# A driver that merges streams by modelled engine times instead of written-out latencies

## The chip, the cores and the metric

The kernel runs on one core of a Trainium2 chip. Its engines are named as in the profile: PE is TensorE (matmuls; PEld is its loading of weights), DVE is VectorE, ACT is ScalarE, POOL is GpSimd, SP is SyncE, which issues most DMAs. The metric is device time in microseconds from start to end of one execution, as a median of several runs.

## The reference

Three layers run on 512 positions of width 1024, in fp32. The first mixes grouped-query attention with a bidirectional gated delta rule; the second and the third are a stick-breaking attention and a differential attention, each with a SwiGLU feed-forward behind it.

```python
def first_block(x, p, ...):
    h = rms_norm(x, norm_pre[i])
    (aq, ak, av, az, dq, dk, dv, db, da, dz, gate_att, gate_dn) = split_cols(h @ w_in[i])
    o_att = gqa_attention(q, k, v)               # q, k normed per head, rotated
    qkv = silu(short_conv(concat([dq, dk, dv]), conv_w[i]))
    o_dn = bidir_gated_deltanet(qd, kd, vd, g, beta)   # chunks of 64, state carried
    mix = (sigmoid(gate_att) * y_att + sigmoid(gate_dn) * y_dn) @ w_out[i]
    x = x + rms_norm(mix, norm_post[i])
    return x + rms_norm(sigmoid(x @ w_ple_gate[i]) * (p[i] @ w_ple_proj[i]), ple_norm[i])

def stick_breaking_attention(q, k, v):           # 16 heads of 64
    z = einsum('bqhd,bkhd->bhqk', q_blk, k) * scale
    log_keep = where(earlier, log_sigmoid(-z), 0.0)
    log_after = cumsum(log_keep, reverse=True) - log_keep
    weight = where(earlier, exp(log_sigmoid(z) + log_after), 0.0)
    return einsum('bhqk,bkhd->bqhd', weight, v)

def differential_attention(q1, q2, k1, k2, v, lam):
    a = softmax(mask(q1 @ k1)) - lam * softmax(mask(q2 @ k2))
    return a @ v

x = x + mixer(rms_norm(x)); x = x + (silu(h @ w_gate) * (h @ w_up)) @ w_down   # twice
```

## The kernel before

Activations stay on chip, with features on partitions and the 512 positions as columns (or the other way round where a stage wants it). A matmul of fp32 accuracy is made of three passes over values split into a high and a low part (hi, lo), so a projection is three times 8 matmuls of 512 columns for each 128 outputs. Weights come by DMA, and ScalarE and VectorE split them into whi and wlo.

The order of the program is made in Python while the kernel is built. Each piece of work (a projection, an attention unit, a chain of the delta rule) is a generator, a stream, and `Driver.run` (L116) merges the streams. The driver has one clock, `drv.t`, which each matmul or transpose moves on by its cost (`mm`, L293; `transpose`, L303). A stream that yields a number is ready again so much later; one that yields an `Event` is ready when the event has been set, at the time in it; one that yields a pool of slots (`self.free["z"]`: PSUM banks for z) waits for a free one. Among the streams the driver takes the one that is ready first, and among equals the one that stands first in the list. The latencies of VectorE and ScalarE are constants, written by hand: SB_LAT1 = 5.0 and SB_LAT2 = 1.2 in the stick-breaking units, CH1 to CH3 = 1.3 in the delta rule's chain, and so on. A scheduler of the framework then places instructions on each engine; an engine runs its instructions in the order that results.

The stages, in order of time: the first block (to about 885 us of the span), the start of the stick-breaking projections (to 921), the stick-breaking units with the rest of their projections (to 1147), the end of the output projection (to 1179), a feed-forward (to 1542), the differential stage (to 1821), a feed-forward.

In the first block, streams project q, k, v of the attention (paq, pak, pv in the trace), z, and dq, dk, dv of the delta rule; `conv` (L831) takes a projection of these out of its PSUM bank on ScalarE (cacc) and runs the short convolution on VectorE; `dn_prep` (L858) transposes the results on TensorE (tr) and multiplies them (kk, kq); `dn_inv` (L959) inverts the triangular matrices; `dn_chain` (L1126) carries the state (kS, wS).

The stick-breaking stage has 48 units, for 8 pairs of heads, 2 heads, and three blocks of keys (b = 2, 1, 0; b = 2 holds two blocks, in 384 columns, b = 1 one in 384, b = 0 one in 512). The `unit` of `stick` (L694) does:

```python
            if prev:
                yield prev["S"]
            yield self.free["z"]
...
                self.mm(zz, kh[:, ks], q[:, P * i:], j == 0, False)
...
            self.split(sh[:, :n], sl[:, :n], t, act=False)
...
            drv.set(me["S"])
            yield SB_LAT1
...
            w = self.work("w")[:, :n]
            nc.scalar.activation(out=w, in_=zz, func=AF.Exp)
            drv.release(self.free["z"], SB_LAT2)
            yield SB_LAT2
```

Called A here are its first matmuls (z from qs with kh and kl, and a mask); then follow Abs, Exp and Ln on ScalarE (L714 to L716, tile t), and on VectorE a sum (L717), sh (L319) and sl (L320). Called B are the matmuls of sh and sl with negones and m_ntri, which add the reversed cumulative sum into z; then Exp on ScalarE gives w (L733), and C are the matmuls po from w and v. The projections of the stage (pv, sb_q, sb_k) are one more stream, last in the list, and the output projection (po0, po1 from ohi and olo) follows them there. In the differential stage, `unit` (L1910) is built in the same manner, with softmax; its output os is transposed on TensorE (otr).

Of the kernel before, what the change touches and what calls it, by code (L numbers as in the profile page):

```python
# [79 lines left out]
class Event:  # L80
    def __init__(self):
        self.t = None
# [14 lines left out]
class Driver:  # L97
# [2 lines left out]

    def __init__(self):
        self.t = 0.0

    def set(self, ev, lat=0.0):
        ev.t = self.t + lat

    def release(self, slots, lat=0.0, n=1):
        slots.free.extend([self.t + lat] * n)  # L110

    def spawn(self, g):

        self.tasks.insert(0, [g, self.t, None])

    def run(self, streams):  # L116
        tasks = self.tasks = [[g, 0.0, None] for g in streams]
        while tasks:
            best = None
            for k, (g, ready, need) in enumerate(tasks):  # L120
                if isinstance(need, Event):
                    if need.t is None:
                        continue
                    ready = max(ready, need.t)
                elif isinstance(need, Take):
                    if len(need.slots.free) < need.n:
                        continue
                    ready = max(ready, sorted(need.slots.free)[need.n - 1])
                key = (max(ready, self.t), k)
                if best is None or key < best[0]:  # L130
                    best = (key, k)
            if best is None:
                raise RuntimeError("streams wait for each other: " + str([(g.__name__, n) for g, _, n in tasks]))
            task = tasks[best[1]]
            self.t = max(self.t, best[0][0])
            g, _, need = task
            if isinstance(need, Take):
                need.slots.free.sort()
                del need.slots.free[:need.n]
            try:  # L140
                v = next(g)
            except StopIteration:
                tasks.remove(task)
                continue
            if isinstance(v, Slots):
                v = Take(v, 1)
            if isinstance(v, (Event, Take)):
                task[1:] = self.t, v
            else:
                task[1:] = self.t + (v or 0.0), None  # L150


class Raw:
# [14 lines left out]
class Net:  # L168
    def __init__(self, ctx, tc, ins, out):
        self.tc = tc  # L170
        self.nc = tc.nc
        self.ins = ins
        self.out = out
        self.drv = Driver()
        self.pre = None
        self.nw = 0

# [57 lines left out]

    def drop(self, n, lat=0.0):

        self.drv.release(self.mem, lat, n)

    def need(self, n):  # L240
        return Take(self.mem, n)
# [16 lines left out]
    def consts(self):  # L258
        nc = self.nc
        self.ident = self.cp.tile([P, P], F32, name="ident")  # L260
        make_identity(nc, self.ident)
# [31 lines left out]
    def mm(self, out, lhsT, rhs, start, stop):  # L293
        n = 1
        for d in rhs.shape[1:]:
            n *= d
        if lhsT.dtype == F32R:
            self.drv.t += max(n * 0.42, 106 if lhsT.shape[-1] == P and lhsT.shape[0] == P else 54) / 1000
        else:
            self.drv.t += max(n * 1.67, 108) / 1000  # L300
        self.nc.tensor.matmul(out, lhsT=lhsT, rhs=rhs, start=start, stop=stop, skip_group_check=True)  # L301

    def transpose(self, out, in_):  # L303
        self.drv.t += 0.109
        self.nc.tensor.transpose(out, in_, self.ident)

    def mm3(self, out, ls, rs, start, stop):
# [14 lines left out]
    def wtile(self, ap, n=1024):  # L322

        nc = self.nc
        with self.tc.high_priority(offset=self.woff):
            st = self.wst.tile([P, 1024], F32, tag="st", name="st")
            nc.sync.dma_start(out=st[:, :n], in_=ap)
            self.nw += 1
            third = self.w3 is not None and self.nw % 4 == 0
            hi = (self.w3 if third else self.whi).tile([P, 1024], F32R, tag="hi", name="whi")  # L330
            lo = (self.w3 if third else self.wlo).tile([P, 1024], F32R, tag="lo", name="wlo")
            self.split(hi[:, :n], lo[:, :n], st[:, :n])
        return hi, lo

    def wtile_big(self, ap):

        nc = self.nc
        parts = []
        with self.tc.high_priority(offset=WBOFF):
            for j in range(2):  # L340
                st = self.work("wbst")
                BQ(nc).dma_start(out=st, in_=ap[:, j * T:(j + 1) * T])
                hi, lo = self.chunk("wbhi", F32R), self.chunk("wblo", F32R)
                self.split(hi, lo, st)
                parts.append((hi, lo))
        return parts

# [778 lines left out]
    def dn_chain(self, S, hh, d):  # L1126
# [13 lines left out]
        for step in range(4):  # L1140
# [4 lines left out]
            if step:  # L1145
# [1016 lines left out]
```

## Time and profile before

| | |
|---|---|
| median of 3 runs | 2192.55 us (2190.63 to 2194.14) |
| the profiled execution | 2189.46 us |
| its span, first to last instruction | 2187.7 us |
| mean granted clock of TensorE | 0.986 |
| busy: PE, DVE, ACT, POOL | 2101.1, 1234.3, 991.6, 115.7 us |
| first block, 0 to 885 us: PE busy | 823.26 us |
| stick-breaking units, 921 to 1147 us: PE busy | 223.89 us |
| differential stage, 1542 to 1821 us: PE busy | 260.69 us |

Busy is the time in which an engine has an instruction under way; matmuls overlap in TensorE's pipeline, so a single matmul's duration (some 0.39 us for 512 columns) is longer than its step to the next. The clock is a share of TensorE's full 2.4 GHz, 0.50 being 1.2 GHz. A row's "<-" in square brackets names what ended the idle time ahead of it.

### The profile page before, as it was taken

How to read it: one execution, taken by the hardware profiler on the slowest of the kernel's cores; microseconds unless marked ns; L12 is line 12 of the kernel's file. 1: busy time of each engine (PE TensorE's matmuls, PEld its weight loads, DVE VectorE, ACT ScalarE, POOL GpSimd, SP SyncE). 2: the span in 40 equal slices, each digit the busy share in tenths (PEclk: the TensorE clock that was granted, in tenths of full speed). 3: DMA queues.
4: the chain of work that ended last, by engine and by line, in shares of the span. 5: the costliest groups of instructions: out<-in, count | busy, mean ns of one | idle time of the engine just before them, and what ended most of it. 6: DMA issues, size and time to landing. Idle time of an engine off the chain costs nothing.

```text
span 2187.7 us, 32571 instructions
## 1 busy us (share of the span) xinstructions
PE 2101.1 (96%) x12830; PEld 1783.9 (82%) x12830; DVE 1234.3 (56%) x2487; ACT 991.6 (45%) x2001; POOL 115.7 (5%) x157
## 2 busy tenths in 40 slices
PE   7999899899999999899999999999999989999999
PEld 6788788778788877788878888888999968888887
DVE  8865774786542546755555444433577765444421
ACT  6556556555632345566664222222466544222211
POOL 2000000000000000000000000000111100000000
PEclk9999999998999999899999999999999999999999
DMA  4221021131324353011103222333211112222332
GB/s 156 75 80 53 32 80 50 46 93 47 117 88 145 130 174 104 20 49 58 48 31 107 96 96 97 94 92 99 91 50 50 57 58 94 95 95 97 92 112 71
DMA packets 73994, 181.68 MB, mean 83 GB/s; under 512 B 24177, under 2 KB 24817, under 8 KB 73841
## 3 DMA queue, kind: packets, MB, share of 16 engines
q1 hardware_dynamic: 72560, 175.40, 25.0%
q0 software_dynamic: 1280, 4.20, 0.6%
q8 instruction: 101, 1.65, 0.3%
q14 instruction: 53, 0.43, 0.1%
HBM read 170.13 MB, written 9.44 MB: 82 GB/s over the span
## 4 chain that ended last, share of the span: by engine, by line
PE 80%; DVE 11%; ACT 4%; issue 2%; POOL 2%; DMA 0%; SPq 0%; POOLq 0%; DVEq 0%; ACTq 0%
PE pg L301 17%; PE pd L301 11%; PE pu L301 11%; PE po L301 9%; PE pb L301 4%; PE pv L301 3%; PE z L301 3%; PE pz L301 3%; PE pk L301 2%; PE wS L301 2%; DVE cacc L845 2%; PE sb_q L301 2%; PE sb_k L301 1%; PE s L301 1%; DVE wlo L320 1%
## 5 line engine op out<-in xcount | busy, mean ns | idle before, releaser
L317 ACT CAST whi<-st 128x1024 fp32r<-128x1024 f32 (+1 forms) x295 | 306.2, 1040 | 787.7 <-issue 343.3
L320 DVE TENSOR_TENSOR wlo<-st,whi 128x1024 fp32r<-128x1024 f32 (+1 forms) x295 | 356.5, 1210 | 281.6 <-ACT whi L317 276.8
L301 PE MATMUL pg<-rlo,whi 128*128 128x512 f32 x352 | 138.7, 394 | 0.0
L301 PE MATMUL pg<-rhi,whi 128*128 128x512 f32 x352 | 138.1, 392 | 0.0
L301 PE MATMUL pg<-rhi,wlo 128*128 128x512 f32 x352 | 138.0, 392 | 0.0
L301 PE MATMUL pd<-mh,wlo 128*128 128x512 f32 x352 | 137.5, 391 | 0.0
L301 PE MATMUL pd<-mh,whi 128*128 128x512 f32 x352 | 137.5, 391 | 0.0
L301 PE MATMUL pd<-ml,whi 128*128 128x512 f32 x352 | 137.5, 391 | 0.0
L301 PE MATMUL pu<-rhi,wlo 128*128 128x512 f32 x352 | 137.2, 390 | 0.0
L301 PE MATMUL pu<-rlo,whi 128*128 128x512 f32 x352 | 137.1, 389 | 0.0
L301 PE MATMUL pu<-rhi,whi 128*128 128x512 f32 x352 | 136.9, 389 | 0.0
L2030 DVE TENSOR_TENSOR sg<-pg,rfm 128x512 f32<-128x512 f32 x44 | 30.4, 692 | 118.4 <-PE pg L301 118.3
L2036 DVE TENSOR_TENSOR m<-pu,sg 128x512 f32<-128x512 f32 x44 | 30.4, 692 | 115.4 <-PE pu L301 115.4
L845 DVE SCALAR_TENSOR_TENSOR cacc<-craw,convw,cacc 128x510 f32<-128x510 f32 (+1 forms) x96 | 70.2, 746 | 17.6 <-ACT cacc L841 16.7
L301 PE MATMUL pv<-whi,rhi 128*128 128x256 f32 x256 | 76.6, 299 | 3.3 <-ACT tmq L1848 2.1
L301 PEld LDWEIGHTS pg<-rhi,wlo 128*128 128x128 f32 x352 | 66.2, 188 | 15.1 <-issue 0.5
L301 PEld LDWEIGHTS pg<-rlo,whi 128*128 128x128 f32 x352 | 66.3, 188 | 15.0 <-issue 0.5
L301 PEld LDWEIGHTS pg<-rhi,whi 128*128 128x128 f32 x352 | 66.2, 188 | 14.5
L301 PEld LDWEIGHTS pd<-ml,whi 128*128 128x128 f32 x352 | 66.2, 188 | 14.3
L301 PEld LDWEIGHTS pd<-mh,wlo 128*128 128x128 f32 x352 | 66.1, 188 | 14.2
L301 PEld LDWEIGHTS pd<-mh,whi 128*128 128x128 f32 x352 | 66.1, 188 | 14.2
L301 PEld LDWEIGHTS pu<-rlo,whi 128*128 128x128 f32 x352 | 66.1, 188 | 14.0
(563 smaller groups left out, 5679.7 us busy)
## 6 DMA issues: line engine op xcount, KB each, us to landing
st<-w_gate SPq DMA_DIRECT2D x44, 512.0 KB, 3.3
st<-w_up SPq DMA_DIRECT2D x44, 512.0 KB, 3.3
st<-w_down SPq DMA_DIRECT2D x32, 512.0 KB, 3.5
st<-w_dn SPq DMA_DIRECT2D x24, 512.0 KB, 3.4
st<-w_out SPq DMA_DIRECT2D x24, 512.0 KB, 3.4
st<-w_down SPq DMA_DIRECT2D x16, 384.0 KB, 3.2
x<-xT SPq DMA_DIRECT2D x16, 256.0 KB, 5.9
st<-w_aq SPq DMA_DIRECT2D x8, 512.0 KB, 3.3
```

Source lines behind the costliest of these rows:

```text
L301: self.nc.tensor.matmul(out, lhsT=lhsT, rhs=rhs, start=start, stop=stop, skip_group_check=True)
L317: nc.scalar.copy(hi, src)
L320: nc.vector.tensor_tensor(lo, src, hi.bitcast(F32), op=ALU.subtract)
L845: nc.vector.scalar_tensor_tensor(out=acc[:, a], in0=raw[:, b], scalar=w[:, s:s + 1], in1=acc[:, a], op0=ALU.mult, op1=ALU.add)
L2030: nc.vector.tensor_tensor(sg, ps, self.rfm, op=ALU.mult)
L2036: nc.vector.tensor_tensor(m, ps, sg, op=ALU.mult)
```

## The change

The driver gets a small model of three engines. `Engines` and `Modelled` wrap the engines of the framework, so that each operation a stream issues on VectorE, ScalarE, GpSimd or a DMA queue goes through `Driver.op`, which estimates when it could start (after its inputs, after the driver's time, in the first gap of its engine that is long enough) and end, by a cost that is linear in the width. The end is kept per tensor (`done`) and per step of a stream (`task.end`, `task.bank_end` for the operations that read PSUM).

`set` then stamps an event with the modelled end of what the step issued, and no longer with the time of the call and a written latency; `release` and `yield number` do likewise. So `drv.set(me["S"])` of a stick-breaking unit, which had the time of the call, now has the modelled end of sl. In `dn_chain` three yields name the tensors that they wait for. The costs of matmuls in `mm` are new, the splitting of weights is modelled as early by 4 us, and `make_identity` uses the unwrapped engines. What is computed stays the same, and so does the number of instructions on PE, DVE, POOL and SP; ACT has two more ACT_TABLE_LOAD, since the sines of the rotary tables now stand between other functions. In the changed kernel nearly all operations of the wrapped engines carry the line of the wrapper, L236.

```diff
     def __init__(self):
         self.t = 0.0
+        self.done = {}
+        self.busy = {e: [] for e in ("vector", "scalar", "gpsimd")}
+        self.end = self.bank_end = 0.0
+        self.early = False
+        self.task = None
+    def place(self, engine, ready, cost):
+        b = self.busy[engine]
+        while b and b[0][1] < self.t - 20:
+            b.pop(0)
+        at = ready
+        for k, (x, y) in enumerate(b):
+            if at + cost <= x:
+                b.insert(k, (at, at + cost))
+                return at
+            at = max(at, y)
+        b.append((at, at + cost))
+        return at
+    def op(self, engine, fn, out, ins):
+        ready = self.t - 4.0 if self.early else self.t
+        for a in ins + ([out] if fn == "accumulate" else []):
+            ready = max(ready, self.done.get(a.tensor.name, 0.0))
...
+            if engine == "vector":
+                cost, more = 0.065 + n / 960, 0.09
+                if fn in ("tensor_scalar", "scalar_tensor_tensor"):
+                    cost += 0.055
+            elif engine == "scalar":
+                cost, more = 0.1 + n / 1220, 0.1
+            else:
+                cost, more = (0.3 + 0.17 * n if fn == "tensor_tensor" else 0.1 + n / 500), 0.05
+            end = self.place(engine, ready, cost) + cost + more
+        self.done[out.tensor.name] = max(end, self.done.get(out.tensor.name, 0.0))
+        if not self.early and self.task is not None:
+            self.task.end = max(self.task.end, end)
+            self.task.has = True
+            if any(a.space == PSUM for a in ins):
+                self.task.bank_end = max(self.task.bank_end, end)
     def set(self, ev, lat=0.0):
-        ev.t = self.t + lat
-
-    def release(self, slots, lat=0.0, n=1):
-        slots.free.extend([self.t + lat] * n)
+        ev.t = max(self.t, self.task.end) if self.task is not None and self.task.has else self.t + lat
+
+    def release(self, slots, lat=0.0, n=1, bank=True):
+        t = self.t + lat
+        if self.task is not None and self.task.has:
+            t = max(self.t, self.task.bank_end if bank else self.task.end)
+        slots.free.extend([t] * n)
...
+            elif v is None or isinstance(v, (int, float)):
+                if v:
+                    task.ready = max(self.t, task.end) if task.has else self.t + v
             else:
-                task[1:] = self.t + (v or 0.0), None
+                for a in v if isinstance(v, tuple) else (v,):
+                    task.ready = max(task.ready, self.done.get(a.tensor.name, 0.0))
...
         if lhsT.dtype == F32R:
-            self.drv.t += max(n * 0.42, 106 if lhsT.shape[-1] == P and lhsT.shape[0] == P else 54) / 1000
+            self.drv.t += max(n / 2400 + 0.013, 0.06)
+        elif lhsT.shape[0] == 32:
+            self.drv.t += 0.033
         else:
-            self.drv.t += max(n * 1.67, 108) / 1000
+            self.drv.t += max(n * 0.00167, 0.11)
+        self.drv.done[out.tensor.name] = self.drv.t + 0.2
...
@@ -1157,7 +1269,7 @@
-                yield CH1
+                yield r
...
-            yield CH2
+            yield (vn, vd) if step < 3 else vn
...
-            yield CH3
+            yield st if step < 3 else CH3
```

The order that results moves on all engines in the first block, the stick-breaking stage and the differential stage. Three places follow.

ScalarE in the stick-breaking stage, before, in the last pair of heads. The tile t of each unit takes Abs (from z), then Exp and Ln (from t); w is the later Exp of a unit:

```order
L714 ACTIVATE t_11546<-z0_11542 128x512
L716 ACTIVATE t_11533<-t_11533 128x384
L715 ACTIVATE t_11546<-t_11546 128x512
L714 ACTIVATE t_11562<-z2_11555 128x384
L716 ACTIVATE t_11546<-t_11546 128x512
L715 ACTIVATE t_11562<-t_11562 128x384
L714 ACTIVATE t_11575<-z1_11571 128x384
L716 ACTIVATE t_11562<-t_11562 128x384
L715 ACTIVATE t_11575<-t_11575 128x384
L716 ACTIVATE t_11575<-t_11575 128x384
L733 ACTIVATE w_11605<-z2_11513 128x384
L733 ACTIVATE w_11613<-z1_11529 128x384
```

The same engine in the changed kernel, in a late pair of heads, "x2" being the Exp and the Ln:

```order
L236 ACTIVATE t_11458<-z2_11451 128x384
L236 ACTIVATE t_11458<-t_11458 128x384 x2
L236 ACTIVATE w_11474<-z2_11451 128x384
L236 ACTIVATE t_11480<-z1_11476 128x384
L236 ACTIVATE t_11480<-t_11480 128x384 x2
L236 ACTIVATE w_11497<-z1_11476 128x384
L236 ACTIVATE t_11503<-z0_11499 128x512
L236 ACTIVATE t_11503<-t_11503 128x512 x2
L236 ACTIVATE w_11521<-z0_11499 128x512
L236 ACTIVATE t_11530<-z2_11523 128x384
L236 ACTIVATE t_11530<-t_11530 128x384 x2
```

Before, Abs, Exp and Ln of up to five units stand between each other, and their w come after; now the four operations of a unit stand together, and the next unit begins behind its w. This holds for all 48 units.

TensorE in the same stage, before, in the last pair of heads (rows of A, by qs, kh and kl, of three units):

```order
L301 MATMUL z2_11513<-qs_11373,kh_11485 128x256
L301 MATMUL z2_11513<-qs_11373,kl_11487 128x256
L301 MATMUL z2_11513<-m_ge_196,neg30_184 128x128
L301 MATMUL z2_11513<-qs_11373,kh_11485 128x128
L301 MATMUL z2_11513<-qs_11373,kl_11487 128x128
L301 MATMUL z2_11513<-m_ge_196,neg30_184 128x128
L301 MATMUL z1_11529<-qs_11373,kh_11485 128x384
L301 MATMUL z1_11529<-qs_11373,kl_11487 128x384
L301 MATMUL z1_11529<-m_ge_196,neg30_184 128x128
L301 MATMUL z0_11542<-qs_11373,kh_11485 128x512
L301 MATMUL z0_11542<-qs_11373,kl_11487 128x512
L301 MATMUL z0_11542<-m_ge_196,neg30_184 128x128
```

and in the changed kernel, in a late pair of heads, a unit's B (sh and sl), its C (po from w), and the A of a later unit:

```order
L408 MATMUL z1_11324<-sh2_11311,negones_225 128x128
L408 MATMUL z1_11324<-sl2_11312,negones_225 128x128
L408 MATMUL z1_11324<-sh2_11311,negones_225 128x256
L408 MATMUL z1_11324<-sl2_11312,negones_225 128x256
L408 MATMUL z1_11324<-sh1_11333,m_ntri_223 128x384
L408 MATMUL z1_11324<-sl1_11334,m_ntri_223 128x384
L408 MATMUL po_11264<-w_11345,v1_10154 128x384
L408 MATMUL z2_11451<-qs_10814,kh_10878 128x256
L408 MATMUL z2_11451<-qs_10814,kl_10880 128x256
L408 MATMUL z2_11451<-m_ge_196,neg30_184 128x128
L408 MATMUL z2_11451<-qs_10814,kh_10878 128x128
L408 MATMUL z2_11451<-qs_10814,kl_10880 128x128
```

Before, the A of several units stand in a row, with their B in a row behind; now B, C and one A alternate. In the changed kernel the A of 24 units stand behind the last matmul of sb_k, before those of 6.

TensorE in the first block, in the second batch of the delta rule, before: dq and dv are projections (from hhi and hlo, the normed input), tr the transpose of dv's earlier result, kk and kq products of dk and dq:

```order
L301 MATMUL dq_2866<-hlo_625,whi_2869 128x512
L301 MATMUL dq_2866<-hhi_624,wlo_2870 128x512
L305 MATMUL tr_2803<-ident_179,dv_2728 128x128 x4
L301 MATMUL kk_2810<-dk_2332 128x128 x4
L301 MATMUL kq_2840<-dq_2456,dk_2332 128x128 x4
L301 MATMUL dv_2908<-hhi_432,whi_2911 128x512
L301 MATMUL dv_2908<-hlo_433,whi_2911 128x512
L301 MATMUL dv_2908<-hhi_432,wlo_2912 128x512
L301 MATMUL dv_2908<-hhi_454,whi_2911 128x512
L301 MATMUL dv_2908<-hlo_455,whi_2911 128x512
```

and in the changed kernel, where 18 matmuls of the projection dv_2862 stand between its first row and the transpose of dv (the rows before these are its first 15):

```order
L413 MATMUL tr_2881<-ident_179,dk_2799 128x128 x4
L408 MATMUL dv_2862<-hhi_687,whi_2865 128x512
L408 MATMUL dv_2862<-hlo_688,whi_2865 128x512
L408 MATMUL dv_2862<-hhi_687,wlo_2866 128x512
L408 MATMUL dec_2899<-gm_2844,m_lt_211 128x512
L408 MATMUL dec_2899<-gm_2846,m_lt_211 128x512
L408 MATMUL dec_2899<-m_lt_211,neg30_184 128x512
L413 MATMUL tr_2914<-ident_179,dv_2717 128x128 x4
L408 MATMUL kk_2921<-dk_2602 128x128 x4
L408 MATMUL kq_2936<-dq_2669,dk_2602 128x128 x4
L408 MATMUL dv_2862<-hhi_696,whi_2865 128x512
```

The transpose of dv and the two products have moved from ahead of the projection to a place inside it.

## Rows read from the trace of the kernel before

**Rows 1.** Table by stage: window, length, busy us of each engine, clock, DMA share, GB/s.

```profile
0.00:885.00 885.00, 823.26 (x6168) 696.56 (x6168) 557.75 (x1228) 455.12 (x1124) 58.89 (x87) 0.98 0.28 91
...
921.00:1147.00 226.00, 223.89 (x1280) 190.90 (x1281) 128.72 (x217) 147.42 (x276) 9.90 (x24) 1.00 0.14 47
...
1179.00:1542.00 363.00, 363.00 (x1590) 298.18 (x1589) 155.84 (x183) 105.05 (x132) 0.00 (x0) 1.00 0.30 95
1542.00:1821.00 279.00, 260.69 (x1880) 243.50 (x1880) 200.44 (x626) 156.65 (x306) 43.81 (x41) 0.98 0.19 62
```

**Rows 2.** Waits of PE in the first block: us in total, times, longest.

```profile
PE dv L301 <- ACT cacc L841: 6.1, 2, 3.1
PE tr L305 <- DVE dk L849: 4.3, 3, 2.8
PE tr L305 <- DVE tmq L1297: 3.2, 3, 1.7
...
PE tr L305 <- DVE dv L849: 2.4, 2, 1.2
```

**Rows 3.** Waits of PE in the differential stage.

```profile
PE otr L305 <- DVE os L1985: 10.7, 5, 2.5
```

**Rows 4.** Groups of ScalarE, whole run, shapes apart: busy us, mean ns.

```profile
L506 ACT ACT_TABLE_LOAD x6 | 7.7, 1283 | 0.9 <-PEq L2152 0.8
```

**Rows 5.** Groups of ScalarE and VectorE in the stick-breaking stage, 384 wide.

```profile
L715 ACT ACTIVATE t<-t 128x384 f32<-128x384 f32 x32 | 16.7, 526 | 0.3
L716 ACT ACTIVATE t<-t 128x384 f32<-128x384 f32 x32 | 16.7, 525 | 0.2
L714 ACT ACTIVATE t<-z 128x384 f32<-128x384 f32 x32 | 15.4, 486 | 5.0 <-PE z L301 5.0
...
L320 DVE TENSOR_TENSOR sl<-t,sh 128x384 fp32r<-128x384 f32 x32 | 17.8, 555 | 0.8
L717 DVE SCALAR_TENSOR_TENSOR t<-z,t 128x384 f32<-128x384 f32 x32 | 17.6, 553 | 18.1 <-ACT t L716 18.1
L319 DVE CAST sh<-t 128x384 fp32r<-128x384 f32 x32 | 11.4, 357 | 0.7
```

**Rows 6.** Timeline near the end of the stick-breaking stage: start, duration, instruction.

```profile
1131.02 0.56 DVE L320 TENSOR_TENSOR sl<-t,sh 128x384 fp32r<-128x384 f32 x1
...
1131.66 0.62 PE L301 MATMUL z<-sh,negones 128*128 128x128 f32 x1
...
1132.59 0.27 PE L301 MATMUL z<-sl,m_ntri 128*128 128x128 f32 x1
...
1132.90 0.49 ACT L733 ACTIVATE w<-z 128x384 f32<-128x384 f32 x1 [2.20 <-PE z L301]
...
1134.29 0.60 ACT L714 ACTIVATE t<-z 128x512 f32<-128x512 f32 x1
...
1137.43 0.69 DVE L320 TENSOR_TENSOR sl<-t,sh 128x512 fp32r<-128x512 f32 x1
...
1139.57 0.22 PE L301 MATMUL z<-sh,negones 128*128 128x128 f32 x1
...
1140.61 0.39 PE L301 MATMUL z<-sl,m_ntri 128*128 128x512 f32 x1
...
1141.04 0.60 ACT L733 ACTIVATE w<-z 128x512 f32<-128x512 f32 x1 [4.82 <-PE z L301]
```

**Rows 7.** Table of the stick-breaking stage, instructions on tile z alone.

```profile
921.00:1147.00 226.00, 81.34 (x512) 70.11 (x512) 28.53 (x48) 49.01 (x96) 1.00 0.14 47
```

**Rows 8.** The same, instructions on tile w alone.

```profile
921.00:1147.00 226.00, 40.25 (x128) 20.23 (x128) 24.23 (x48) 1.00 0.14 47
```

**Rows 9.** Table behind two waits of dv: granted clock before the DMA share.

```profile
249.20:252.40 3.20, 3.20 (x9) 2.42 (x9) 3.20 (x6) 0.03 (x1) 0.00 (x0) 0.50 0.00 0
414.00:418.00 4.00, 3.69 (x16) 3.07 (x17) 3.70 (x7) 1.33 (x3) 0.26 (x1) 1.00 0.00 0
```

More of the change, by code (lines that the diff above doesn't have):

```diff
@@ new lines, in op @@
+    def op(self, engine, fn, out, ins):
+        ready = self.t - 4.0 if self.early else self.t
+        for a in ins + ([out] if fn == "accumulate" else []):
+            ready = max(ready, self.done.get(a.tensor.name, 0.0))
+        width = lambda a: math.prod(a.shape[1:])
+        if fn == "dma_start":
+            end = ready + 2.2
+            if engine == "gpsimd":
+                self.place(engine, ready, 0.55)
+        else:
+            n = max([width(out)] + ([width(ins[0])] if fn in ("tensor_reduce", "reduce_sum") else []))
+            if engine == "vector":
[4 more added lines that the diff above has]
+                cost, more = 0.1 + n / 1220, 0.1
+            else:
+                cost, more = (0.3 + 0.17 * n if fn == "tensor_tensor" else 0.1 + n / 500), 0.05
[6 more added lines that the diff above has]
+                self.task.bank_end = max(self.task.bank_end, end)
@@ L116, in run @@
     def run(self, streams):
-        tasks = self.tasks = [[g, 0.0, None] for g in streams]
+        tasks = self.tasks = [Task(g, 0.0) for g in streams]
         while tasks:
             best = None
-            for k, (g, ready, need) in enumerate(tasks):
+            for k, task in enumerate(tasks):
+                need, ready = task.need, task.ready
                 if isinstance(need, Event):
@@ L130, in run @@
                 if best is None or key < best[0]:
-                    best = (key, k)
+                    best = (key, task)
             if best is None:
-                raise RuntimeError("streams wait for each other: " + str([(g.__name__, n) for g, _, n in tasks]))
-            task = tasks[best[1]]
+                raise RuntimeError("streams wait for each other: " + str([(t.g.__name__, t.need) for t in tasks]))
+            task = self.task = best[1]
             self.t = max(self.t, best[0][0])
-            g, _, need = task
+            need = task.need
             if isinstance(need, Take):
@@ L139, in run @@
                 del need.slots.free[:need.n]
+            task.has = False
             try:
-                v = next(g)
+                v = next(task.g)
             except StopIteration:
@@ L144, in run, with __init__, __getattr__, issue @@
                 continue
+            finally:
+                self.task = None
             if isinstance(v, Slots):
                 v = Take(v, 1)
+            task.need, task.ready = None, self.t
             if isinstance(v, (Event, Take)):
-                task[1:] = self.t, v
-            else:
-                task[1:] = self.t + (v or 0.0), None
+                task.need = v
+            elif v is None or isinstance(v, (int, float)):
+                if v:
+                    task.ready = max(self.t, task.end) if task.has else self.t + v
+            else:
+                for a in v if isinstance(v, tuple) else (v,):
+                    task.ready = max(task.ready, self.done.get(a.tensor.name, 0.0))
+class Task:
+    def __init__(self, g, ready):
+        self.g, self.ready, self.need = g, ready, None
+        self.end = self.bank_end = 0.0
+        self.has = False
+class Modelled:
+    def __init__(self, engine, name, drv):
+        self._engine, self._name, self._drv = engine, name, drv
+    def __getattr__(self, fn):
+        real = getattr(self._engine, fn)
+        if not callable(real):
+            return real
+        def issue(*args, **kw):
+            res = real(*args, **kw)
+            aps = [a for a in args if hasattr(a, "tensor")]
+            out = kw["out"] if "out" in kw else aps.pop(0) if aps else None
+            if out is not None:
+                ins = aps + [v for k, v in kw.items() if k not in ("out", "accum_out") and hasattr(v, "tensor")]
+                self._drv.op(self._name, fn, out, ins)
+                if "accum_out" in kw:
+                    self._drv.done[kw["accum_out"].tensor.name] = self._drv.done[out.tensor.name]
+            return res
+        return issue
+class Engines:
+    def __init__(self, nc, drv):
+        self.real = nc
+        self.tensor = nc.tensor
+        for name in ("vector", "scalar", "gpsimd", "sync"):
+            setattr(self, name, Modelled(getattr(nc, name), name, drv))
 class Raw:
@@ L343, in wtile_big @@
                 hi, lo = self.chunk("wbhi", F32R), self.chunk("wblo", F32R)
+                self.drv.early = True
                 self.split(hi, lo, st)
+                self.drv.early = False
                 parts.append((hi, lo))
```

15 lines of the change are left out of this document (9 added, 6 removed).

## The prediction

> **What bounds the kernel now.** I read a table by stage first [rows 1]. TensorE is busy almost everywhere, so the kernel is bound by matmuls, and a change of order that keeps the matmuls can at best win back TensorE's idle time. The table says where that lies: the first block has 885.00 - 823.26 = 61.7 us of it, the stick-breaking stage 226.00 - 223.89 = 2.1 us, the differential stage 279.00 - 260.69 = 18.3 us. The feed-forward stages have none: 363 us for some 1590 matmuls, 0.228 us each. So the first block and the differential stage can gain, and the stick-breaking stage can only lose: 48 units pass there through TensorE, ScalarE and VectorE in turn, all of it behind other matmuls.
>
> Then I read the waits of TensorE. In the first block much is spent on start, norms and stage ends, which no merging moves. What the order could move is shown by four rows [rows 2]: a projection that waits for the convolution's ScalarE step to free its bank (6.1), and transposes that wait for VectorE (4.3, 3.2, 2.4), together 16.0 us. In the differential stage five transposes of the output wait 10.7 us for VectorE [rows 3].
>
> **The change, part by part.** The instructions on TensorE, VectorE, GpSimd and SyncE are the same in number; ScalarE gets two more table loads, 1.28 us each [rows 4], between the rotary tables and the sigmoids in the middle of the first block. ScalarE is busy for 455 of 885 us there [rows 1] and TensorE has projections to do, so I cost them at nothing; with that cover gone they are 2.6 us. All the rest is order. The first rows on TensorE and the last stages (both feed-forwards, most of the output projection) don't move at all: 0 us.
>
> *Stick-breaking.* A unit is: matmuls A into z; Abs, Exp, Ln on ScalarE; three operations on VectorE that end in sl; matmuls B into z; Exp (w) on ScalarE; matmuls C. The next unit's A waits for the event S, which the unit sets after issuing sl. Before, S got the time at which the step was issued, so several units are open at once, and ScalarE's rows interleave them. In the changed kernel S gets the modelled end of sl. ScalarE's rows then read, for all 48 units, Abs, Exp, Ln, w of one unit and only then the Abs of the next. ScalarE works in the order of its rows, so the next Abs can't start before w has ended, and w can't start before B, which needs sl. The units become one chain: Abs to sl, B, w, next Abs.
>
> Its price, from operations that were timed in this stage [rows 5, 6]. For a 384-wide unit the six operations up to sl are 0.486 + 0.526 + 0.525 + 0.553 + 0.357 + 0.555 = 3.00 us bare; I take 3.1 with the gaps between them. From sl's end (1131.02 + 0.56) to the first B matmul are 0.08 us, from there to the start of w 1132.90 - 1131.66 = 1.24, and w takes 0.49: 4.91. For the 512-wide unit, the last of the run, Abs to the end of sl is 1137.43 + 0.69 - 1134.29 = 3.83, then 0.08, then 1141.04 - 1139.57 = 1.47, then 0.60: 5.98. A head has two of the first and one of the second: 15.80 us, 5.27 a unit.
>
> Whether that costs anything depends on what TensorE has to do meanwhile. In the rows of the changed kernel the projections (pv, sb_q, sb_k) fill 24 of the steps, with 4.1 to 8.6 us of matmuls between one B and the next. But with units this far apart the projections run ahead and end early: 24 units start after the last sb_k matmul, where in the kernel before 6 do. What fills the last 24 steps is the units' own matmuls and 48 matmuls of the output projection. The units' matmuls took 81.34 us (z) and 40.25 us (C) for 48 units [rows 7, 8], 2.53 us a unit at most, since matmuls overlap and these two rows count the overlap with neighbours; with the overlap out, some 2.3. So TensorE has 24 x 2.3 to 2.53 + 48 x 0.228 [rows 1] = 66 to 72 us of work in a chain of 24 x 5.27 = 126 us. Loss: 54 to 60 us; I take **+59**, nearer to the lower count of work, as the two rows were taken in a stage that is crowded with matmuls. Ends: +45 (no gaps anywhere, chain 4.7 a unit) and +68 (0.3 us more a unit).
>
> In the first 24 steps the cover is thin where it is 4.1 to 4.8 us (12 of them): the chain from the end of B to the next B needs about 3.1 or 3.8, plus w and its start (0.8), and the projections' evacuations stand on the same two engines. I take a third of a microsecond each, **+4**, ends 0 and +12.
>
> *The clock in that stretch.* TensorE will be some 50% busy there, with a wait of half a microsecond to a microsecond and one of about 2 us in each step. After waits of such a length the granted clock has fallen in one case and not in another. The two waits of dv for its bank, 6.1 us together and 3.1 the longest [rows 2], ended at 248.2 and 414.3 us: behind the first the clock was at 0.50 (1.2 GHz) for some 3 us, behind the second it stayed at 1.00 (2.4 GHz) [rows 9]. At half clock only B lengthens the chain, by its own start-to-start time: 1132.59 - 1131.66 = 0.93, or 1140.61 - 1139.57 = 1.04 us [rows 6]; A and C have room. All 24 units at half clock would be +23. I take about half, **+11**, ends 0 and +23. The Trainium skill ("TensorE: Matmul & The Clock Gate", section "HAM oscillation — how this bites in real kernels") describes a loop in which matmuls come in bursts with waits between them, and each burst ran at the lower clock; by that it would be the full +23 and the time 2257. The two stretches of [rows 9] agree with that in one case of two, so I stay at half.
>
> *First block.* Here the model does good. At the place shown above, the wait of TensorE for dv's transpose and then for a free bank came in a row; in the changed kernel 18 matmuls of the next projection, 18 x 0.228 = 4.1 us, stand ahead of that transpose, which covers its wait. The attention units are spread in the same way between projections, which flattens VectorE's load. Of the 16.0 us of [rows 2] I count two thirds as won, 11 us, and with them two or three stretches of half clock behind such waits, which cost half of their 3 us each [rows 9]: **-15**. The ends are -30 (half of all the idle time of the block) and +8: counted at 0.228 us a wide matmul, the chains of the DeltaNet state now leave 1.1 us of other work between dependent steps, where there were 1.6 to 2.7, which may not cover their latency.
>
> *Differential stage.* Its units aren't chained in that way. The work between a unit's last product and the transposes of its output rises for most heads (5 to 6.5 us to 6.5 to 10 us) and falls to nothing at the last: **-3**, ends -8 and +5.
>
> **Sum.** The profiled execution took 2189.5 us (span 2187.7). 2189.5 + 59 + 4 + 11 - 15 - 3 = **2245.5**, say 2245. It lies 3.1 us under the median shown, 2192.55, which is no more than the runs' own spread, so I leave it at 2245. Runs of this kernel differ by less than 0.2%, 4.4 us; less than that is told as no change.
>
> **The rivals.**
> - *The clock stays low* through the whole tail and the first block wins nothing, since the waits come back at other places: 2189.5 + 59 + 4 + 23 = 2275. The mixed rows on the clock allow it, and a wait removed in a stage that is short of VectorE often comes back. Chance 0.25.
> - *Only the wait for w counts.* If ScalarE's order in the tail cost no more than the exp that C waits for, half of the units wait about 0.9 us (w and its start) each, 22 us, and the first block and the differential stage give 18 back: 2193, no change. It would need Abs to sl, over 3 us, to be hidden behind 2.3 us of work; the rows speak against it. Chance 0.04.
> - *Faster.* One mechanism: the chain of the tail is no longer than TensorE's work there, because neighbouring units overlap on ScalarE and VectorE after all. Then the stage stays at 226 us and the gains alone remain: 2189.5 - 18 = 2171. It decides when a unit takes less than (69 + 18)/24 = 3.6 us; six operations in a row take 3.0 without B and w, and the order allows no overlap. A first block that won all its 30 us and a differential stage that won 8 would still not reach it with the chain at 5.27. Chance 0.07.
> - The forecast, 0.64.
>
> **Range.** All ends together would be 2196 and 2305; 8 in 10 I see between 2214 (chain at its low end, clock mostly up, block at -25) and 2280 (the first rival and a little). Faster 0.07, same 0.04, slower 0.89.
>
> **What the changed profile would show.** Right: the stick-breaking stage some 70 us longer, its first part (to the last sb_k) about as fast as now, its second at 5 to 6 us a unit, with TensorE waiting for sl and for w, and VectorE and ScalarE idle in turn; the clock below 1.00 in part of it; waits of tr for dv, dk and tmq and of dv for cacc smaller in the first block; feed-forwards unchanged. Wrong: waits on TensorE in the stage of less than 20 us (then the chain overlaps), or new waits for kS, wS and N in the first block of over 10 us (then the gain there is a loss), or a clock that is low all through.

## The result and the profile after

The changed kernel takes 2260.86 us (median of 4 runs, 2246.91 to 2265.10), the kernel before 2193.35 us (4 runs, 2190.63 to 2194.45). The ratio is 1.0299, with a 95% interval of 1.0251 to 1.0346. The profiled execution, 2246.91 us with a span of 2245.2 us, is the fastest of the four, which matters below.

The table by stage of the changed kernel, cut at its own borders (first A at 918.3 us, last sb_k at 1073.6, last B at 1190.1, first feed-forward at 1230.9, second at 1878.6); its columns are those of [rows 1]:

```profile
0.00:881.00 881.00, 821.79 (x6169) 694.81 (x6170) 562.44 (x1229) 462.11 (x1127) 60.42 (x87) 0.98 0.29 92
918.00:1074.00 156.00, 156.00 (x904) 135.17 (x903) 86.71 (x132) 97.83 (x167) 7.60 (x18) 1.00 0.20 65
1074.00:1191.00 117.00, 93.10 (x370) 63.22 (x370) 44.48 (x82) 55.11 (x106) 0.00 (x0) 0.83 0.01 5
1191.00:1231.00 40.00, 38.90 (x153) 30.21 (x154) 22.26 (x28) 17.67 (x25) 0.00 (x0) 0.90 0.29 92
1231.00:1594.00 363.00, 363.00 (x1591) 298.24 (x1590) 156.01 (x184) 105.15 (x132) 0.00 (x0) 1.00 0.31 95
1594.00:1879.00 285.00, 261.57 (x1880) 243.52 (x1880) 203.54 (x627) 158.21 (x307) 46.53 (x41) 0.97 0.19 61
```

The loss is almost all in one row, 1074 to 1191: TensorE starts 370 matmuls there in 117 us, where the row above has 904 in 156, and its clock is 0.83. By stages, in the two profiled executions: to the first A 918.3 after 921.0 before (-2.7); from there to the first feed-forward 312.6 after 258.1 (+54.5); from feed-forward to feed-forward 647.7 after 642.0 (+5.7); the end equal. The sum is the +57.5 of the spans.

The waits of TensorE in the stick-breaking stage, total, times, longest:

```profile
PE po L408 <- ACT w L236: 10.6, 17, 0.7
PE z L408 <- DVE t L236: 9.0, 11, 1.6
PE z L408 <- DVE sh L236: 2.8, 4, 0.9
PE z L408 <- DVE sl L236: 0.6, 2, 0.3
```

TensorE waits for w and, for B, for t: hardly ever for sl. One step of the chain in the timeline (start, duration) shows why:

```profile
1097.53 0.56 DVE L236 SCALAR_TENSOR_TENSOR t<-z,t 128x384 f32<-128x384 f32 x1 [2.89 <-ACT t L236]
1098.12 0.36 DVE L236 CAST sh<-t 128x384 fp32r<-128x384 f32 x1
...
1098.14 0.33 PE L408 MATMUL z<-sh,negones 128*128 128x128 f32 x1 [0.64 <-DVE t L236]
...
1098.52 0.56 DVE L236 TENSOR_TENSOR sl<-t,sh 128x384 fp32r<-128x384 f32 x1
...
1099.13 0.44 PE L408 MATMUL z<-sl,m_ntri 128*128 128x384 f32 x1
1099.61 0.49 ACT L236 ACTIVATE w<-z 128x384 f32<-128x384 f32 x1 [2.11 <-PE z L408]
1099.99 0.59 ACT L236 ACTIVATE t<-z 128x512 f32<-128x512 f32 x1
...
1100.15 0.91 PE L408 MATMUL po<-w,v 128*128 128x384 f32 x2 [0.58 <-ACT w L236]
```

B's first matmuls read sh and sl of earlier key blocks and need only that t has been read out of z, so they run beside sh and sl; only B's last matmul needs the new sl. (In the units of b = 2, which hold two blocks, B starts with the new sh.) From the end of sl to w this unit takes 1099.61 - 1099.08 = 0.53 us. The next Abs follows w at 1099.99, as the order said. From the w at 1077.47 us to that at 1122.55, ten steps at full clock, a unit takes 45.08 / 10 = 4.51 us; over all 24 steps, to 1190.72, 4.72 us.

### The profile page after: what moved, and what is told of

It is laid out like the page before. It is cut to its first block, busy times and chain, and to the rows that moved or that the text cites. A ratio compares the mean times of both kernels' runs of the same rounds, so it can differ in the third digit from the quotient of the medians.

```text
span 2245.2 us, 32519 instructions
## 1 busy us (share of the span) xinstructions
PE 2131.8 (95%) x12830; PEld 1792.7 (80%) x12830; DVE 1246.1 (56%) x2487; ACT 1009.0 (45%) x2003; POOL 119.7 (5%) x157
## 4 chain that ended last, share of the span: by engine, by line
PE 75%; DVE 12%; ACT 6%; issue 3%; POOL 2%; DMA 0%; SPq 0%; POOLq 0%; DVEq 0%; ACTq 0%
PE pg L408 17%; PE pd L408 11%; PE pu L408 11%; PE po L408 8%; PE pb L408 4%; PE z L408 3%; PE pv L408 2%; PE pz L408 2%; PE wS L408 2%; PE sb_q L408 2%; PE sb_k L408 2%; DVE wlo L236 2%; ACT t L236 2%; DVE cacc L236 1%; PE s L408 1%
## 5 line engine op out<-in xcount | busy, mean ns | idle before, releaser
L236 ACT CAST whi<-st 128x1024 fp32r<-128x1024 f32 (+1 forms) x295 | 305.9, 1039 | 752.1 <-issue 323.6
L236 DVE TENSOR_TENSOR wlo<-st,whi 128x1024 fp32r<-128x1024 f32 (+1 forms) x295 | 356.1, 1209 | 268.3 <-ACT whi L236 259.4
L236 DVE TENSOR_TENSOR sg<-pg,rfm 128x512 f32<-128x512 f32 x44 | 30.4, 692 | 118.4 <-PE pg L408 118.4
L236 DVE TENSOR_TENSOR m<-pu,sg 128x512 f32<-128x512 f32 x44 | 30.4, 692 | 115.4 <-PE pu L408 115.4
L236 DVE SCALAR_TENSOR_TENSOR t<-z,t 128x384 f32<-128x384 f32 (+1 forms) x48 | 28.9, 602 | 118.0 <-ACT t L236 117.9
L408 PEld LDWEIGHTS pu<-rhi,whi 128*128 128x128 f32 x352 | 66.1, 188 | 14.0
```

The source lines that it names most:

```text
L236: res = real(*args, **kw)
```

## The experiments

Twelve runs, each beside runs of the kernel before on the same chip. Stage times are from each run's own profile.

**1. S at the call again**, in the stick-breaking unit of the changed kernel alone.

```diff
-            drv.set(me["S"])
+            me["S"].t = drv.t
```

> The changed kernel, but event S of a stick-breaking unit gets the driver's time at the call again. Theory: the chain Abs to w of one unit after another, with 24 units behind the last projection, is the whole loss of that stage (258.1 us from its first A to the feed-forward before, 312.6 changed), so it comes back to 256 to 262 us with under 4 us of waits, and the time falls by some 52 us below the changed kernel's profiled 2247, to about 2193. Rival: the projections run ahead because of the model's other times (release of z, B's delay), whatever S holds: the stage stays above 295 us, the time above 2230.

2209.37 us (ratio 1.0070, 1.0046 to 1.0094). The stage takes 258.3 us, as before. Its waits on TensorE, whole:

```profile
PE po L408 <- ACT w L236: 0.9, 3, 0.4
PE z L408 <- DVE sl L236: 0.2, 1, 0.2
```

So this one stamp is the whole loss of the stage. But the time stays 16 us above before, where some 2193 us had been expected: the first A comes at 932.5 us (918.3 in the changed kernel's profile), with the same order in the first block, and the differential stage keeps its 5.6 us. More on that in run 3.

**2. The chain put into the kernel before**, by written latencies.

```diff
-SB_LAT1 = 5.0
+SB_LAT1 = 3.4
-            drv.set(me["S"])
+            drv.set(me["S"], SB_LAT1)
```

> The kernel before, its driver without a model, with one thing put in: S of a stick-breaking unit is stamped 3.4 us late and B follows after the same 3.4 us, so that the units stand one behind the other on ScalarE as in the changed kernel. 15 units then start behind the last projection (24 in the changed kernel, 6 before). Theory: the loss is (chain of a unit less TensorE's work in it) times the units behind the last projection, 15 x (4.5 - 2.3) less 11 us of output projection, 22 us, with some microseconds of low clock: 2212 to 2225. Rival 1: a chained unit loses its time in every one of the 48 steps: 2240 or more. Rival 2: the chain is harmless without the rest of the model: under 2200.

2228.52 us (1.0165, 1.0151 to 1.0179); the stage takes 294.4 us, +36.3. The time is above the theory's 2212 to 2225 and below the first rival's 2240. The steps behind the last projection take 73.9 us for matmuls of some 15 x 2.3 + 11 = 46, a loss of 28 (with the clock at 0.85 there). Of the other 8, 2.7 stand behind the last B, where the stage's end takes 41.2 us in place of 38.5; the rest is lost where steps have cover.

**3. The model in the first block alone**, and **4. everywhere but there**: `op` returns at once where it is off, and the three tensor yields become CH1 to CH3 again.

```diff
+        if not self.on:
+            return
...
+            net.drv.on = False
             net.stick(x, R, 0, R2, [last])
```

> The changed kernel with the model switched off behind the first block, so that events, releases and numbers there work as before (the new matmul costs stay). Theory: the stick-breaking and the differential stage return to their times of before (258 and, feed-forward to feed-forward, 642 us), and only the first block's small gain is left: 2184 to 2191. Rival: the first block's gain was luck of the profiled run, or the differential stage is longer by the new matmul costs: 2192 to 2200.

> The changed kernel with the model switched off in the first block only. Theory: the stages add up, so the first block takes its 885 us of before, the stick-breaking stage 312 and the differential stage some 6 more than before: 2249 in a run like the profiled one, up to 2268 where the clock is lower. Rival: the stages act on each other through what the first block leaves behind, and the time is under 2235.

Run 3: 2211.43 us (1.0077, 1.0058 to 1.0096), not the 2184 to 2191 expected. Run 4: 2252.79 us (1.0276, 1.0263 to 1.0290), within its forecast, with 312.9 and 647.8 us in the two later stages. Run 3's profile is 21.6 us longer than that of before: 11.5 of it stand ahead of the first A (932.6 us), 2.4 in the stick-breaking stage and 7.6 in the differential stage; the last two are those of run 7. So the model in the first block costs time in most executions (of run 3's six, four took 2211 to 2213 us and two 2202 and 2203), and the changed kernel's profile was a lucky one. The table of run 3, in the stretch where the chain of the delta rule's third batch ends and the fourth batch's inversion runs (32x32 matmuls up to 581 us, then 64x64 ones, between the matmuls of the projection pb):

```profile
550.00:560.00 10.00, 9.60 (x78) 9.04 (x77) 7.92 (x30) 6.42 (x25) 0.00 (x0) 1.00 0.01 2
560.00:570.00 10.00, 5.01 (x26) 3.31 (x25) 5.19 (x19) 7.92 (x31) 2.01 (x2) 0.92 0.12 41
570.00:580.00 10.00, 9.64 (x130) 6.92 (x130) 5.63 (x9) 4.82 (x12) 0.00 (x0) 0.50 0.32 118
580.00:590.00 10.00, 10.00 (x97) 7.70 (x96) 1.22 (x1) 4.65 (x11) 0.00 (x0) 0.50 0.01 2
590.00:600.00 10.00, 10.00 (x57) 8.82 (x56) 0.66 (x3) 4.38 (x15) 0.00 (x0) 0.54 0.15 52
600.00:610.00 10.00, 10.00 (x83) 9.55 (x82) 6.76 (x26) 6.13 (x23) 0.00 (x0) 1.00 0.01 2
```

TensorE waits for half of 560 to 570, the clock falls to 0.50 and stays there for 30.7 us. In the changed kernel's profile the low stretch at the same place is 6.8 us, 24 us shorter; at half clock 24 us of matmuls cost 12, and the first A differs by 14. Ahead of the first A the clock was at 0.50 for 78 us in all in runs 1, 3 and 5, for 48 before and for 44 in the changed kernel's profile. The 30 us more than before are worth up to 15, an estimate, and the loss is 11.5, so the lower clock alone can account for it.

**5. Extra matmuls in the tail**, which A overwrites.

```diff
+REP = 5
...
+                if hp >= 4 and j == 0:
+                    for _ in range(REP):
+                        nc.tensor.matmul(zz, lhsT=kh[:, ks], rhs=q[:, P * i:], start=True, stop=False, ...)
```

> The changed kernel, with five extra matmuls ahead of the A of each of the last 24 stick-breaking units, which write the same bank and are overwritten by A itself; they stand where TensorE waits. Theory: the low clock in the tail (48 us of it in the changed kernel's profile, 9 us of time) comes from TensorE's waits, so with less idle time the clock stays at 1.00 there, a unit takes 4.5 us, the stage (first A to feed-forward, 312.6 us) shortens to 302 to 307, and the runs of one kernel differ less. Rival: the extra matmuls only lengthen each unit, since B stands behind them: 315 us or more.

2258.03 us (1.0300, 1.0285 to 1.0315). The table of the tail, to hold against the row 1074 to 1191 above:

```profile
1090.00:1204.00 114.00, 101.60 (x492) 73.74 (x490) 44.83 (x83) 55.35 (x106) 0.00 (x0) 0.96 0.02 5
```

With the waits partly filled the clock is 0.96 in place of 0.83 (it fell at 1195 us, for 17 us); the last 24 units take 4.58 us each in place of 4.72, and the stage 309.2 us, 3.4 less, short of the 302 to 307 expected. The chain itself is the loss; the clock is a small part.

**6. The model with the matmul costs of before**, and **7. the new costs alone**, in the kernel before.

```diff
-            self.drv.t += max(n / 2400 + 0.013, 0.06)
+            self.drv.t += max(n * 0.42, 106 if lhsT.shape[-1] == P and lhsT.shape[0] == P else 54) / 1000
```

> The changed kernel with the matmul costs of before in the driver, the model otherwise whole. Theory: the model's times cause the loss, so the stick-breaking stage stays above 305 us and the whole between 2245 and 2268. Second question, the differential stage (feed-forward to feed-forward 642 us before, 648 changed, 650 with the model off but the new costs): if the new costs lengthen it, it goes back to 640 to 644 here; if not, it stays at 646 to 650.

> The kernel before with the new matmul costs and nothing else of the change. Theory: the costs alone do no harm in the first block and in the stick-breaking stage (885 and 258 us), and lengthen the differential stage by 6 to 8 us, as the run with the model off there did: 2196 to 2202. Rival: the costs carry none of it, and the differential stage stays at 642 us: 2190 to 2195.

Run 6: 2253.24 us (1.0281, 1.0258 to 1.0304). The stick-breaking stage takes 316.4 us, as the theory said; the differential stage 652.7 us, which is neither of the two answers. Run 7: 2200.58 us (1.0039, 1.0024 to 1.0054), as expected: 260.4 and 650.0 us in the two stages. So the new costs alone lengthen the differential stage by 8 us, the model with the old costs by 10.6, both together by 5.7. In run 7 the wait of [rows 3] grows by 2.0 us, with one of po beside it, and the clock is lower, 0.96 where [rows 1] has 0.98:

```profile
PE otr L307 <- DVE os L1987: 12.7, 4, 4.2
PE po L303 <- DVE os L1987: 2.4, 4, 0.7
```

```profile
1545.00:1833.00 288.00, 267.26 (x1885) 248.49 (x1884) 202.47 (x627) 159.58 (x307) 44.22 (x41) 0.96 0.18 61
```

It stood at 0.50 for 24 us of the stage, for 14 before; these 10 us are worth some 5 of the 8.

**8. The chain and the inversion of the delta rule by written latencies**, the rest of the first block by the model.

```diff
+OLD = ("dn_chain", "dn_inv")
...
-        if not self.early and self.task is not None:
+        if not self.early and self.task is not None and self.task.g.__name__ not in OLD:
...
-                yield r
+                yield CH1
```

> As the run with the model in the first block alone (2211 us, first block 895 us), but there the streams of the delta rule's chain and inversion keep their written latencies. Theory: the first block loses because in the modelled order the chain of the third batch and the inversion of the fourth stand almost without projections between them, TensorE waits there, and the clock stays at 0.50 for some 30 us; with projections between the steps again the block takes 876 to 886 us and the whole 2194 to 2203. Rival: the loss comes from the attention and convolution streams, and the block stays above 890 us.

2201.93 us (1.0044, 1.0027 to 1.0061): the first A comes at 924.0 us, 8.6 sooner than in run 3, and the low stretch lasts 20.5 us. With the chain and the inversion by written latencies most of the first block's loss is gone. The run does not tell the two apart.

**9. Run 3 with the old matmul costs**, and **10. run 8 with them.**

> The model in the first block alone, and the matmul costs of before everywhere. Theory: the stages add, so the stick-breaking and the differential stage take 258 and 642 us as before, and the first block with what follows to the first A takes 919.5 us as in the run of the model with old costs (921.0 before): 2188, or up to 2198 in executions in which the low clock lasts longer in the first block. Rival: the first block's order is worse than before in most executions: 2200 or more.

> As the run before it, and with the delta rule's chain and inversion by their written latencies. Theory: without the bare chain the first block neither gains nor loses more than a few microseconds: first A at 917 to 925 us, 2186 to 2196, and the executions differ by less than with the modelled chain. Rival: what the first block loses lies in the other streams, and it takes 925 us or more to the first A, 2197 or more.

Run 9: 2186.80 us, ratio 0.9968 (0.9956 to 0.9980), a little faster than before, and 1 us below the 2188 of the theory. First A at 919.1 us, with the chain and the inversion by the model; the stages behind it are back:

```profile
919.00:1177.00 258.00, 255.83 (x1420) 217.23 (x1421) 148.62 (x242) 162.22 (x296) 9.88 (x24) 1.00 0.17 56
...
1540.00:1819.00 279.00, 260.71 (x1880) 243.49 (x1879) 200.40 (x626) 156.53 (x306) 43.76 (x41) 0.98 0.19 62
```

Run 10: 2190.78 us, 0.9991 (0.9982 to 1.0000): first A at 920.4, no difference from before. Its executions spread over 8.1 us, run 9's over 9.9. Runs 3, 8, 9 and 10 belong together: up to the first A the modelled chain and inversion lose 8.6 us against written latencies with the new matmul costs, and win 1.3 with the old ones. So the first block's loss needs both, the model and the new costs; with the costs alone (run 7) the first A comes at 922.0.

**11. Run 3 with twelve extra matmuls** of 512 columns at the end of the third batch's chain, overwritten by the transposes behind them.

```diff
+REP = 12
...
         tp = self.bank("z", "tro")
+        if S["b"] == 2 and hh == 0:
+            for _ in range(REP):
+                nc.tensor.matmul(tp, lhsT=self.neg30, rhs=self.o_att[0][0], start=True, stop=False, ...)
```

> The kernel with the model in the first block alone (2211 us, first A at 932.6 us, clock 0.50 from 568 to 599 us), with twelve extra 512-wide matmuls, 2.7 us, at the end of the third batch's chain, into a bank that the transposes behind them overwrite. Theory: the clock falls there because TensorE waited in the chain and for the branch's input, so with the wait filled the long stretch goes or shrinks below 10 us, and the first A comes at 917 to 925 us in spite of the extra work. Rival: it stays low because of what TensorE does behind it, the inversion's 32x32 matmuls, and the first A comes at 932 us or later.

2210.37 us (1.0083, 1.0065 to 1.0101), no better than run 3. The two rows around the inversion:

```profile
568.00:577.00 9.00, 6.98 (x94) 5.13 (x93) 4.99 (x11) 4.15 (x16) 1.01 (x1) 1.00 0.41 144
577.00:598.00 21.00, 20.60 (x187) 15.96 (x186) 3.99 (x5) 11.68 (x31) 0.00 (x0) 0.52 0.12 40
```

The clock stayed up until 577.8 us and then fell for 20.5 us, inside the inversion; the first A came at 931.4, nearly where the rival had it. The theory falls as it stood: the wait filled was not the only cause, though some 2 us of waits were left in 568 to 577. What TensorE does in the inversion isn't the whole cause either: the changed kernel's profile has the same order there as run 3 and the same 3.9 us of idle time in the 10 us ahead of it, and its clock was up from 570.8 us on. What holds the clock down stays open.

**12. The chain with less room between units**: run 2 with 1.6 in place of 3.4.

> As the run with the chain put into the kernel before (2228.5 us; stick-breaking stage 294.4 us from first A to feed-forward, 15 units behind the last projection), with 1.6 us in place of 3.4, so that the 48 units still stand one behind the other on ScalarE, but only 7 of them behind the last projection (6 before). Theory: what costs is the chain without cover at the end, and with projections spread over nearly all steps (some 4.9 us of matmuls a step against a chain of 4.5) the stage takes 262 to 275 us, the whole 2195 to 2210. Rival: a chained unit costs wherever it stands, and the stage stays at 285 us or more, the whole at 2220 or more.

2239.61 us (1.0211, 1.0194 to 1.0229), the rival's number: the stage takes 308.3 us though only 7 units stand behind the last projection. The times of w on ScalarE:

```profile
1023.06 0.49 ACT L733 ACTIVATE w<-z 128x384 f32<-128x384 f32 x1 [1.97 <-PE z L301]
...
1027.15 0.49 ACT L733 ACTIVATE w<-z 128x384 f32<-128x384 f32 x1 [2.11 <-PE z L301]
...
1031.96 0.60 ACT L733 ACTIVATE w<-z 128x512 f32<-128x512 f32 x1 [2.50 <-PE z L301]
...
1036.51 0.49 ACT L733 ACTIVATE w<-z 128x384 f32<-128x384 f32 x1 [2.46 <-PE z L301]
```

The step is 4.1 to 4.8 us in the middle of the stage too. In the 1.6 us that the driver allows it places too little beside a step, and the rest of the projections stands in lumps: three times 15.7 to 17.6 us pass without a w. The other 44 steps take 4.80 us on average, with some 3.7 us of matmuls each (an estimate: the 219.6 us from first A to last B before, less 51 in the lumps and 6 ahead of the first w). That makes 44 x 1.1 = 48 of the 50 us lost. So what costs is any step of the chain with fewer matmuls beside it than the chain takes, wherever it stands. The units behind the last projection are the changed kernel's case of that, not the rule.

## Why the prediction was right, and where it was not

The direction and the place were right, and the median lies in the range, but partly by errors that cancel. Point by point, against the profiled execution where a stage is meant:

- **The units become one chain on ScalarE.** Shown: the order of w and Abs in the timeline, and run 1, which takes the whole loss of the stage away with one stamp (312.6 to 258.3 us).
- **The chain's price, +59: mis-sized.** The step that failed is the time from the end of sl to w, 1.32 us for b = 1 and 2 and 1.55 for b = 0, in which all of B was put behind sl. In the units of b = 1 and 0 B needs t and old sh and sl, and only its last matmul the new sl, so most of B runs beside sh and sl, and the times are 0.53 and 0.60 us; in those of b = 2, where B needs the new sh too, it is 0.87. The rows read for it came from two units: the sl that ends at 1131.58 in [rows 6] is that of b = 1, while the B at 1131.66 and the w at 1132.90 are those of b = 2, whose sl had ended at 1130.71. A unit takes 4.51 us at full clock and not 5.27, and 24 of them 108 us. With the 66 us of matmuls that the lower count gave, the loss is 42 us.
- **The first 24 steps, +4:** 155.3 us for some 219.6 - 66 = 154 us of work (219.6 us were first A to last B before): under 2 us.
- **The clock in the tail, +11:** between the ten full-clock steps and all 24, 24 x (4.72 - 4.51) = 5 us, and a few more behind the last B, where the clock is 0.90. Run 5, in which it was up longer, gained 3.4. The mean over the tail is 0.83, so two thirds of it ran at 1.00. The loop that the Trainium skill describes ("TensorE: Matmul & The Clock Gate", section "HAM oscillation — how this bites in real kernels"), in which every burst runs at the lower clock, is thus not what happened here. But that loop waits longer than TensorE ever did in this stage, 1.6 us, so the trace does not contradict the page; the forecast applied it to shorter waits.
- **The first block, -15: wrong.** The profile has -2.7, and the same order in runs 1, 3 and 5 has +11.5 to +13.6. The wait of dv for its bank and that of dv's transpose are gone, as forecast, and that of dk fell from 4.3 to 3.4 us; that of tmq rose from 3.2 to 4.8. The step that failed is "I count two thirds as won, 11 us": TensorE's idle time in the block fell from 61.7 us to 881.00 - 821.79 = 59.2 only, since other waits came. That the chains of the state "may not cover their latency" had been kept for the bounds alone: the waits for wS are new, 6.7 us in all, and that of dec grew from 2.2 to 7.3 us. N waited before, too. Before, in the first block:

```profile
PE N L301 <- issue: 6.1, 3, 3.0
...
PE dec L301 <- DVE gm L906: 2.2, 3, 1.4
```

  and in the changed kernel:

```profile
PE dec L408 <- DVE gm L236: 7.3, 5, 3.7
...
PE tr L413 <- DVE tmq L236: 4.8, 2, 2.8
PE N L408 <- issue: 4.1, 3, 2.4
PE wS L408 <- issue: 3.5, 1, 3.5
...
PE wS L408 <- ACT vn L236: 1.7, 3, 0.9
```

  Behind the chain comes the long stretch of half clock of run 3, which no term had; the forecast counted on two or three stretches of 3 us fewer. Runs 3 and 8 to 10 show that the block's loss takes the modelled chain and inversion together with the new matmul costs; the change was costed as if only the model mattered.
- **The differential stage, -3: wrong in sign.** +5.7. The wait of [rows 3] fell from 10.7 to 6.3 us, as forecast, but other waits came (tp for VectorE, po for at), which I had not counted. Run 7 shows that the new matmul costs are enough to lengthen the stage, and run 6 that the model is, too; no term of the forecast had either.
- **Sum.** 42 + 2 + 8 (the stage measured 54.5), in place of 74, -3 in place of -15 and +6 in place of -3 give about 2245 for the profiled execution, which is where the forecast stood. That it agrees with the profiled execution is luck: the stick-breaking stage was put some 20 us too high, the two others 21 too low. The median is 14 us above that execution. Its executions have clocks of 0.967 to 0.970, the profiled one 0.976; runs 1, 3 and 5 make it likely that the difference is the long stretch in the first block, but it isn't shown, since no trace of those executions exists.

## What to carry to other kernels

An event that releases the next unit must say when the next unit may be *placed*, not when the previous one is done: a driver that stamps it with the modelled end of a chain serialises units that could have been open at once, and filling TensorE's waits afterwards won back only 3.4 us here (run 5). Give the merger several units in flight, and compare each step's cover in matmuls with the time of its chain on the other engines; where the cover is shorter, the difference is lost (runs 2 and 12). A model of the times can help (5 us in run 9), but it is worth trying stage by stage and cost by cost: in the first block the model lost time with one set of matmul costs and won some with another.

## What the runs showed of the hardware

During the inversion of the delta rule TensorE showed no idle time in run 3 from 580 us on, 10.00 us busy of 10, and the granted clock still stayed at 0.50 up to 599 us. In the kernel before the same inversion ran at 1.00 (575 to 595 us), with 9.3 to 9.5 us busy of 10. A row that is full does not mean that the clock is up; at half clock the same matmuls fill more of it. Nor did the order alone decide: in the changed kernel's profile, with the order of run 3 and the same 3.9 us of idle time in the 10 us ahead, the inversion took 12.9 us, all but its first 1.7 us at 1.00; in run 3 it took 21.3, all at 0.50. And executions of one program differed by 18 us, 2246.9 to 2265.1, with clocks from 0.976 down to 0.967.
